# Seven products for eight: more mixed pairs in the second FFN, with their weight sums made during the first FFN

## The chip, the cores and the metric

The kernel runs on one core of one Trainium2 chip. The metric is the device time of one execution in microseconds (us). The engines are called PE (TensorE, matrix multiplies), PEld (its weight load), DVE (VectorE), ACT (ScalarE), POOL (GpSimd) and SP (SyncE, which issues most of the loads here).

## The reference, cut to what matters

One layer of a decoder on 256 tokens and 16 meta tokens, in fp32, with a model width of 2048. The change touches the last step of it, the second FFN:

```python
def swiglu(x, w_gate, w_up, w_down):
    return (jax.nn.silu(x @ w_gate) * (x @ w_up)) @ w_down
...
        h = h + 0.5 * swiglu(u, ffn1_w_gate[l], ffn1_w_up[l], ffn1_w_down[l])
        ... # projections, sparse attention, short convolution, merge
        u = rms_norm(h, ffn2_norm_g[l])
        h = h + 0.5 * swiglu(u, ffn2_w_gate[l], ffn2_w_up[l], ffn2_w_down[l])

    return h[:, N_META:]
```

`w_gate` and `w_up` are 2048 x 5632, `w_down` is 5632 x 2048. All weights arrive in fp32 from device memory, 4 bytes each.

## The kernel before, in words

**Three matmuls for one product.** PE works on rounded numbers (float32r). So each fp32 block of weights is split into a rounded part `whi` (made by ACT) and the rest `wlo` (DVE: the raw block minus `whi`), and each activation block likewise. A product is then a *trio* of matmuls: high times high, high times low, low times high. In the second FFN the activations (128 tokens) are PE's stationary operand and the weights, 512 columns wide, are the moving one.

**The stream of weights.** `Stream` holds all weights in the order of their use. A *raw tile* is 128 x 2048 fp32 (1 MB), loaded by SP into one of three buffers. `add` cuts it into *subs* of at most 1024 columns. `next` walks one sub further on PE. For sub number n it first has sub n + 3 split (`split`: ACT, then DVE), then runs the work whose turn has come (`later(fn, lag)`: the lag counts in subs), and then hands over the blocks of sub n. `whi` and `wlo` have four buffers each, so the split of a sub waits until PE has read the sub four places ahead of it. Since the program is written out in this order and each engine works through its own queue in order, this loop sets what stands behind what on ACT and DVE.

**The second FFN** (`ffn_tokens`) goes in two groups of 6 and 5 column blocks (`GROUPS`; 512 columns each). In a group, a *gate and up unit* f takes the 16 row blocks (k) of its 512 columns of gate and up, in 8 *pairs* of k. An ordinary pair is one raw tile, two subs, and 8 products (2 k, 2 token halves j, gate or up), so 24 matmuls. The products add up in four PSUM banks. A unit is followed, early in the next unit, by `gather` (sums from PSUM, then Silu on ACT), `times` (the product with up), `turn_blocks` (32 x 32 transposes on DVE), `move_blocks` (the blocks go out to device memory and back in another order, through POOL's queue), and `split_blocks` (the result into `mid`, high and low). The last unit of a group turns by `turn_columns` on DVE alone. After a group's units, `tokens` multiplies `mid` with the down weights, 512 output columns at a time (`d`), and `add` adds to the residual `ht`.

**Mixed pairs.** A pair named in `MIXED` is done as a 2 x 2 block product by Strassen and Winograd's scheme: 7 products instead of 8, so 21 matmuls instead of 24, for sums of the blocks on both sides. The sums of activations (`combos`, into `comb`) are made once. The sums of weights are made by DVE as the tile passes (`part`: two differences ahead of sub a, a sum and a difference ahead of sub b). The pair is then four subs, a to d, of 1024, 1024, 1024 and 512 columns. Four of the seven products add up in four more banks (`m`), which are the banks of the unit before, and `spread` adds these into `u` after the last mixed pair. Before, pairs 3 and 5 are mixed in every gate and up unit but the first, which has only 5; down has none.

Of the kernel before, what the change touches and what calls it, by code (L numbers as in the profile page):

```python
# [15 lines left out]
P = 128  # L16
# [49 lines left out]
MIXED = (3, 5)  # L66
# [3 lines left out]
class Stream:  # L70
# [66 lines left out]
    def part(self, raw, name):  # L137

        sub, add = self.nc.vector.tensor_sub, self.nc.vector.tensor_add
        b11, b12, b22, b21 = (raw[:, i * HALF : (i + 1) * HALF] for i in range(4))  # L140
# [49 lines left out]
def tile_decoder_layer(  # L190
# [50 lines left out]
    gu = down = 0  # L241
    for n in GROUPS:
        for i in range(gu, gu + 8 * n):
            if i % 8 in MIXED[i < 8 :]:
                st.add_mixed(wgu2[i])
            else:
                st.add(wgu2[i], 4, 512)
        chunks(wd2, down, down + 4 * n, 512)
        gu, down = gu + 8 * n, down + 4 * n
# [9 lines left out]
    ssq = [const.tile([P, T], F32, name=f"ssq{i}") for i in range(2)]  # L259
    R = const.tile([P, T], F32, name="R")  # L260
    R2 = const.tile([P, T], F32, name="R2")
# [96 lines left out]
    def quads(c, m, x, mixed, n, after_mixed):  # L358
# [5 lines left out]
        for i in range(n):  # L364
            k = 2 * i
            if i in mixed:
                s = [None, *(lambda part, q=q, i=i: mixed[i](q, part) for q in range(4))]
                plan.append([
                    [(c[1, 1], s[4], 0), (c[1, 0], of(k + 1, 1), 1)],
                    [(m[1], of(k, 1), 0), (m[5], s[1], 1)],  # L370
# [3 lines left out]
            else:  # L374
                plan.append([
                    [(c[j, q], of(k + u, j), q ^ u) for j in (1, 2) for q in ((0, 1), (1, 0))[u]] for u in range(2)
                ])
        flat = [id(p[0]) for steps in plan for unit in steps for p in unit]
        at = 0
        for i, units in enumerate(plan):  # L380
            for unit in units:
                blocks = [st.next()] + st.rest()
                for ps, xx, b in unit:
                    trio(ps, xx, blocks[b], id(ps) not in flat[:at], id(ps) not in flat[at + 1 :])
                    at += 1
            if i == max(mixed):
                after_mixed()
# [110 lines left out]
    def ffn_features():  # L498
# [3 lines left out]
        with tc.tile_pool(name="ffn1", bufs=2, reuse_waits="tile") as fp:  # L502
# [15 lines left out]

            two = [aux_tile(f"start{i}") for i in range(2)]
# [35 lines left out]
    def ffn_tokens():  # L555

        with ExitStack() as pools:
# [6 lines left out]
            comb = fp.tile([P, len(MIXED), 4, 2, P], F32R, name="comb")  # L564
            mixed = {i: lambda q, part, n=n: comb[:, n, q, part] for n, i in enumerate(MIXED)}
            late["junk"] = lambda: u[:, 0]

            def combos(n, i):
                y = st.mix[:, :HALF].rearrange("p (b j t) -> p b j t", b=2, j=2)
                z = st.mix[:, HALF : 2 * HALF].rearrange("p (q t) -> p q t", q=4)  # L570
                x = act[:, 2 * i : 2 * i + 2, :, LATER + META :].bitcast(F32).rearrange("p b i (j t) -> p b i j t", j=2)
# [5 lines left out]
                split_into(comb[:, n, :, 0], comb[:, n, :, 1], z)  # L577

            late["mt"] = lambda: fp.tile([P, 4, SEQ], F32, name="mt", bufs=2)
# [18 lines left out]
            def gather(c, s):  # L598
# [44 lines left out]
            for c, n in enumerate(GROUPS):  # L643
# [26 lines left out]
                if n % 2:  # L670
                    mm_tile(), mm_tile()
# [665 lines left out]
```

## Time and profile before

| | |
|---|---|
| median of 3 runs | 2132.63 us (2132.28 to 2132.64) |
| the profiled execution | 2132.57 us, its span 2130.8 us |
| granted PE clock | 1.0 |
| PE, DVE, ACT busy | 2123.0, 1418.4, 995.8 us |
| moved by DMA | 407.03 MB, 191 GB/s over the span |
| first FFN | up to about 796 us of the span |
| second FFN | from 1419 us on |

Read it so: busy time is the sum of the recorded durations on an engine. Matmuls overlap in the record (one lasts 389 ns with 512 columns, but the next starts after 227 ns), so PE's time is read from the distance of starts. A row of the timeline has the start, the duration, engine, line, operation, output and inputs, and in brackets how long the engine was idle before and who released it.

### The profile page before, as it was taken

The page shows a single profiled execution, that of the slowest core. Times are in us where ns is not written, and L with a number is a line of the kernel's source. Part 1 is how long each engine was busy: PE and PEld are TensorE (multiplying, and loading weights), DVE is VectorE, ACT ScalarE, POOL GpSimd, SP SyncE. Part 2 cuts the span into 40 slices and gives each one's busy share as a digit, 9 for nine tenths or more (in the row PEclk, how much of TensorE's full clock was granted, in tenths as well). Part 3 has the DMA queues.
Part 4 walks back from the last instruction along what each step waited for, and adds up shares of the span by engine and source line. Part 5 has one row for each costly group of instructions (what it writes and reads, how often), then busy time and mean ns, then how long its engine had stood idle before and what let it go on. Part 6 is the DMA issues. An engine that isn't in the chain of part 4 may idle for free.

```text
span 2130.8 us, 31133 instructions
## 1 busy us (share of the span) xinstructions
PE 2123.0 (100%) x12839; PEld 1909.7 (90%) x12839; DVE 1418.4 (67%) x1885; ACT 995.8 (47%) x1237; POOL 34.8 (2%) x73
## 2 busy tenths in 40 slices
PE   9999999999999999999999999999999999999999
PEld 9999999999999998799988888887888888888887
DVE  7555544455555556677677477898888854788863
ACT  6444433344444445455544444445555533455542
POOL 0000000000000000000000000000000000000000
PEclk9999999999999999999999999999999999999999
DMA  7554555555555555445455555555666655566664
GB/s 263 188 179 178 179 178 178 178 178 178 179 178 179 178 176 176 171 160 171 160 187 195 197 185 198 190 187 203 229 223 217 219 191 193 205 227 227 223 198 141
DMA packets 59935, 407.03 MB, mean 191 GB/s; under 512 B 7057, under 2 KB 7825, under 8 KB 12433
## 3 DMA queue, kind: packets, MB, share of 16 engines
q1 hardware_dynamic: 55872, 393.51, 53.5%
q0 software_dynamic: 3344, 10.49, 1.5%
q8 instruction: 100, 1.64, 0.3%
q10 hardware_dynamic: 576, 1.05, 0.1%
q14 instruction: 43, 0.34, 0.0%
HBM read 398.20 MB, written 6.82 MB: 190 GB/s over the span
## 4 chain that ended last, share of the span: by engine, by line
PE 97%; DVE 1%; DMA 1%; ACT 0%; issue 0%; SPq 0%; ACTq 0%
PE pd L322 4%; PE pd L320 4%; PE pd L321 4%; PE pg L321 4%; PE pu L321 4%; PE pu L322 4%; PE pg L322 4%; PE pg L320 4%; PE pu L320 4%; PE pd L349 4%; PE pd L348 4%; PE pd L350 4%; PE three L355 3%; PE three L356 3%; PE three L354 3%; PE pgt L350 3%
## 5 line engine op out<-in xcount | busy, mean ns | idle before, releaser
L129 DVE TENSOR_TENSOR wlo<-raw,whi 128x1024 fp32r<-128x1024 f32 (+1 forms) x749 | 909.5, 1219 | 664.8 <-ACT whi L128 661.0
L128 ACT ACTIVATE whi<-raw 128x1024 fp32r<-128x1024 f32 (+1 forms) x749 | 786.9, 1055 | 965.5 <-PE pd L321 146.2
L320 PE MATMUL pd<-mid,whi 128*128 128x272 f32 x704 | 201.7, 286 | 0.0
L321 PE MATMUL pd<-mid,whi 128*128 128x272 f32 x704 | 201.7, 286 | 0.0
L322 PE MATMUL pd<-mid,wlo 128*128 128x272 f32 x704 | 201.7, 286 | 0.0
L320 PE MATMUL pu<-act,whi 128*128 128x272 f32 x672 | 192.6, 287 | 0.0
L321 PE MATMUL pu<-act,whi 128*128 128x272 f32 x672 | 192.5, 287 | 0.0
L322 PE MATMUL pu<-act,wlo 128*128 128x272 f32 x672 | 192.5, 287 | 0.0
L320 PE MATMUL pg<-act,whi 128*128 128x272 f32 x672 | 192.5, 286 | 0.0
L321 PE MATMUL pg<-act,whi 128*128 128x272 f32 x672 | 192.5, 286 | 0.0
L322 PE MATMUL pg<-act,wlo 128*128 128x272 f32 x672 | 192.5, 286 | 0.0
L348 PE MATMUL pd<-whi,mid 128*128 128x512 f32 x352 | 136.9, 389 | 0.0
L349 PE MATMUL pd<-wlo,mid 128*128 128x512 f32 x352 | 136.9, 389 | 0.0
L350 PE MATMUL pd<-whi,mid 128*128 128x512 f32 x352 | 136.9, 389 | 0.0
L320 PEld LDWEIGHTS pd<-mid,whi 128*128 128x128 f32 x704 | 132.6, 188 | 0.0
L321 PEld LDWEIGHTS pd<-mid,whi 128*128 128x128 f32 x704 | 132.6, 188 | 0.0
L322 PEld LDWEIGHTS pd<-mid,wlo 128*128 128x128 f32 x704 | 132.6, 188 | 0.0
L320 PEld LDWEIGHTS pu<-act,whi 128*128 128x128 f32 x672 | 126.6, 188 | 0.0
L321 PEld LDWEIGHTS pg<-act,whi 128*128 128x128 f32 x672 | 126.6, 188 | 0.0
L322 PEld LDWEIGHTS pg<-act,wlo 128*128 128x128 f32 x672 | 126.6, 188 | 0.0
L320 PEld LDWEIGHTS pg<-act,whi 128*128 128x128 f32 x672 | 126.6, 188 | 0.0
L321 PEld LDWEIGHTS pu<-act,whi 128*128 128x128 f32 x672 | 126.6, 188 | 0.0
(299 smaller groups left out, 4216.3 us busy)
## 6 DMA issues: line engine op xcount, KB each, us to landing
raw<-in_wgu_dram SPq DMA_DIRECT2D x174, 1024.0 KB, 4.8
raw<-in_wd_dram SPq DMA_DIRECT2D x88, 1024.0 KB, 4.8
raw<-in_wcv_dram SPq DMA_DIRECT2D x24, 1024.0 KB, 4.8
raw<-in_wgc_dram SPq DMA_DIRECT2D x24, 1024.0 KB, 4.8
raw<-in_wga_dram SPq DMA_DIRECT2D x24, 1024.0 KB, 4.9
raw<-in_wo_dram SPq DMA_DIRECT2D x16, 1024.0 KB, 4.8
raw<-in_wqi_dram SPq DMA_DIRECT2D x8, 1024.0 KB, 4.8
raw<-in_wq_dram SPq DMA_DIRECT2D x8, 1024.0 KB, 4.8
```

What stands on the lines that cost most here:

```text
L128: nc.scalar.activation(hi[:, :n], raw, AF.Copy)
L129: nc.vector.tensor_sub(lo[:, :n], raw, hi[:, :n].bitcast(F32))
L320: nc.tensor.matmul(ps, whi, xhi, start=first, stop=False)
L321: nc.tensor.matmul(ps, whi, xlo, start=False, stop=False)
L322: nc.tensor.matmul(ps, wlo, xhi, start=False, stop=last)
L348: nc.tensor.matmul(ps, xhi, whi, start=k + i == 0, stop=False)
L349: nc.tensor.matmul(ps, xhi, wlo, start=False, stop=False)
L350: nc.tensor.matmul(ps, xlo, whi, start=False, stop=k + i == n - 1)
L354: nc.tensor.matmul(ps, x(0), w[0], start=first, stop=False)
L355: nc.tensor.matmul(ps, x(0), w[1], start=False, stop=False)
L356: nc.tensor.matmul(ps, x(1), w[0], start=False, stop=last)
```

## The change

1. In gate and up, pairs 1, 3 and 5 are mixed (before: 3 and 5). The first unit still mixes only pair 5. That makes 31 mixed pairs there, before 21.
2. The sums of weights of these 31 pairs are made during the first FFN. A `job` loads the raw tile through POOL's queue, DVE makes four sums in place (one after each of four subs), and POOL's queue stores the tile to a tensor `made` in device memory. A job starts every 7 subs, from sub 24 on. In the second FFN such a pair then comes as two raw tiles: three blocks of the weights as they are (0.75 MB; subs of 1024 and 512 columns) and the made tile (1 MB; two subs of 1024). `part` is no longer called for it.
3. Down is done by `quads` too, two column blocks at a time, with the four mixed products in the other four banks. Pairs 4, 6 and 8 of 12 are mixed in the first group, pairs 4 and 7 of 10 in the second, with the sums of weights made on the way (`part`). That is 2 x 3 + 2 x 2 = 10 mixed pairs. The sums of activations for them are made by `down_combos` about 21 subs after the unit that made these rows. `gather_down` and `half_to` take the place of `add`.
4. To make room, `s`, `xt` and a second `mt` are gone. `gather` writes into `few`, which is the storage of `ssq`, `R` and `R2`; it adds both token halves in one instruction of 1024 columns, before in two of 512. One of the four sums of activations of a mixed pair is written over the block it replaces, so `combos` splits its result in two pieces of 128 and 384 columns, before in one of 512.
5. In the last unit of down, the last pair takes its products bank by bank.

```diff
-MIXED = (3, 5)
+MIXED = 1, 3, 5
+FIRST_MIXED = 5,
+JOBS_FROM, JOBS_EVERY = 24, 7
+DOWN_MIXED = {6: (4, 6, 8), 5: (4, 7)}
...
+            if i % 8 in (FIRST_MIXED if i < 8 else MIXED):
+                made.append((i, scratch.tile([P, RAW], F32, name=f"made{i}")))
+                st.add(wgu2[i][:, HALF:], 3, 512)
+                st.add(made[-1][1], 4, 512)
...
+                if i in DOWN_MIXED[n]:
+                    st.add_mixed(wd2[down])
+                else:
+                    st.add(wd2[down], 4, 512)
...
+            def job(i, to, at):
+                box = {}
+                def load():
+                    box["x"] = fp.tile([P, RAW], F32, name="made", bufs=3)
+                    nc.gpsimd.dma_start(box["x"], wgu2[i])
...
+                st.later(load, at)
+                for n in range(4):
+                    st.later(lambda n=n: sums(n), at + JOBS_EVERY + n)
+                st.later(lambda: nc.gpsimd.dma_start(to, box["x"]), at + JOBS_EVERY + 4)
+            for at, (i, to) in enumerate(made):
+                job(i, to, JOBS_FROM + at * JOBS_EVERY)
...
-            def gather(c, s):
-                for j in (1, 2):
-                    nc.vector.tensor_add(s[:, j - 1], c[j, 0], u[:, j - 1])
+            def gather(x, c, box):
+                s = box["s"] = few.rearrange("p a t -> p (a t)")[:, :1024].rearrange("p (j c) -> p j c", j=2)
+                nc.vector.tensor_add(s, x, u[:, :2])
...
+                        for q, i in enumerate(i for i in DOWN_MIXED[n] if i // 2 == f):
+                            st.later(lambda i=i, n=n: down_combos(DOWN_MIXED[n].index(i), i), 21 + q)
...
-                for d in range(D // 512):
-                    pd = {j: mm_tile(f"pd{j}") for j in (1, 2)}
-                    tokens(pd, lambda k, j, part: mid[:, k, part, (j - 1) * P : j * P], 4 * n)
+                for d in (0, 2):
+                    x, c, m = banks()
+                    now = {i: down_sum(q, i) for q, i in enumerate(DOWN_MIXED[n])}
...
+                    quads(c, m, middle_tokens, now, 2 * n, after, g and d)
+                    st.later(lambda d=d, x=x, c=c, g=g: gather_down(d, x, c, g == 1))
```

DVE's queue at the start of the third gate and up unit of the first group, before: the four splits are those of subs 0 to 3 of the new unit, then come the sums from PSUM (`s`, `u`) of the unit that has just ended, the split of sub 4, `times`, the split of sub 5, the transposes, and sub 6, which is the first of a mixed pair (pair 3).

```order
L129 TENSOR_TENSOR wlo<-raw,whi 128x1024 x4
L600 TENSOR_TENSOR s<-three,u 128x512
L600 TENSOR_TENSOR s<-one,u 128x512
L602 TENSOR_TENSOR u<-three,u 128x512
L602 TENSOR_TENSOR u<-two,u 128x512
L129 TENSOR_TENSOR wlo<-raw,whi 128x1024
L608 SCALAR_TENSOR_TENSOR s<-u,rcol,s 128x512 x2
L129 TENSOR_TENSOR wlo<-raw,whi 128x1024
L614 STREAM_TRANSPOSE xt<-s 128x4x4x32 x2
L143 TENSOR_TENSOR mix<-raw 128x512
```

The same place on DVE in the changed kernel: subs 2 to 5 are now those of mixed pair 1.

```order
L132 TENSOR_TENSOR wlo<-raw,whi 128x1024 x3
L132 TENSOR_TENSOR wlo<-raw,whi 128x512
L665 TENSOR_TENSOR few<-three,u 128x1024
L667 TENSOR_TENSOR u<-one,u 128x512
L667 TENSOR_TENSOR u<-two,u 128x512
L132 TENSOR_TENSOR wlo<-raw,whi 128x1024
L674 SCALAR_TENSOR_TENSOR few<-u,rcol,few 128x512 x2
L132 TENSOR_TENSOR wlo<-raw,whi 128x1024
L682 STREAM_TRANSPOSE mt<-few 128x4x4x32 x2
L132 TENSOR_TENSOR wlo<-raw,whi 128x1024 x3
```

The rows keep their order, the split of sub 3 is half as wide, the first two sums are one, and the subs behind them are shorter on PE (1024, 512, 1024 and 1024 columns for 6, 3, 6 and 6 matmuls; before 12 each).

DVE at the start of the fifth unit of the first group, in the changed kernel: `mix` and the two rows after it are `down_combos`, between the splits of subs 1 and 2 of the unit. Before, nothing stood there, as in the third unit.

```order
L132 TENSOR_TENSOR wlo<-raw,whi 128x1024 x2
L624 TENSOR_TENSOR mix<-mid 128x512
L625 TENSOR_TENSOR mix<-mix 128x128
L626 TENSOR_TENSOR mix<-mix 128x128
L627 TENSOR_TENSOR mix<-mix 128x128
L628 TENSOR_TENSOR mix<-mix 128x128
L432 TENSOR_TENSOR mid<-mix,mid 128x128
L432 TENSOR_TENSOR below<-mix,below 128x3x128
L132 TENSOR_TENSOR wlo<-raw,whi 128x1024
L132 TENSOR_TENSOR wlo<-raw,whi 128x512
L665 TENSOR_TENSOR few<-three,u 128x1024
```

The sums of activations now stand ahead of the splits of subs 2 and 3 and of the sums from PSUM.

DVE at the start of down in the first group, before: from the split of sub 5 of the first down block on.

```order
L129 TENSOR_TENSOR wlo<-raw,whi 128x1024
L457 STREAM_TRANSPOSE mt<-s 32x2x4x32 x8
L129 TENSOR_TENSOR wlo<-raw,whi 128x1024
L457 STREAM_TRANSPOSE mt<-s 32x2x4x32 x8
L129 TENSOR_TENSOR wlo<-raw,whi 128x1024
L409 TENSOR_TENSOR mid<-mt,mid 128x4x256
L129 TENSOR_TENSOR wlo<-raw,whi 128x1024 x8
```

The same place in the changed kernel, where sub 8 is the first of mixed pair 4.

```order
L132 TENSOR_TENSOR wlo<-raw,whi 128x1024
L480 STREAM_TRANSPOSE mt<-few 32x2x4x32 x8
L132 TENSOR_TENSOR wlo<-raw,whi 128x1024
L480 STREAM_TRANSPOSE mt<-few 32x2x4x32 x8
L132 TENSOR_TENSOR wlo<-raw,whi 128x1024
L432 TENSOR_TENSOR mid<-mt,mid 128x4x256
L146 TENSOR_TENSOR mix<-raw 128x512
L147 TENSOR_TENSOR raw<-raw 128x512
L132 TENSOR_TENSOR wlo<-raw,whi 128x1024
L150 TENSOR_TENSOR mix<-mix,raw 128x512
L151 TENSOR_TENSOR mix<-raw,mix 128x512
L132 TENSOR_TENSOR wlo<-raw,whi 128x1024
```

Behind the transposes and the split of `mid`, the sums of weights of pair 4 now stand ahead of the splits of subs 8 and 9.

More of the change, by code (lines that the diff above doesn't have):

```diff
@@ L139, in part @@
         sub, add = self.nc.vector.tensor_sub, self.nc.vector.tensor_add
-        b11, b12, b22, b21 = (raw[:, i * HALF : (i + 1) * HALF] for i in range(4))
+        b12, b11, b22, b21 = (raw[:, i * HALF : (i + 1) * HALF] for i in range(4))
         t3, t2, t4 = (self.mix[:, i * HALF : (i + 1) * HALF] for i in range(3))
@@ L385, in quads @@
                     at += 1
+                blocks = [] if unit else blocks
             if i == max(mixed):
@@ L630, in split_blocks @@
                     split_into(hi, lo, x)
+            turns = [0]
             def banks():
[L633 to L641 removed]
@@ L643, in ffn_tokens @@
[L643 to L659 removed]
+                sides = []
@@ new lines, in banks, with out_columns @@
+                for _ in range(2):
+                    one, two = mm_tile("one"), mm_tile("two")
+                    sides.append((aux_tile("three"), one, two))
+                x, one, two = sides[turns[0] % 2]
+                c = {(1, 0): x[:, 0], (2, 0): x[:, 1], (1, 1): one, (2, 1): two}
+                y, six, seven = sides[1 - turns[0] % 2]
+                turns[0] += 1
+                return x, c, {1: y[:, 0], 5: y[:, 1], 6: six, 7: seven}
+            def out_columns(d, j):
+                queue = nc.gpsimd if st.n_loaded < len(st.loads) else (nc.sync, nc.scalar)[j - 1]
+                queue.dma_start(out[j - 1, :, d * 512 : (d + 1) * 512], ht[d][:, j - 1])
@@ new lines, in half_to, with gather_down @@
+            def half_to(to, x):
+                nc.vector.scalar_tensor_tensor(to, x, 0.5, to, op0=ALU.mult, op1=ALU.add)
+            def gather_down(d, x, c, last):
+                if not last:
+                    half_to(ht[d], x)
+                for j in (1, 2):
+                    for q in (0, 1) if last else (1,):
+                        half_to(ht[d + q][:, j - 1], c[j, q])
+                        if last:
+                            out_columns(d + q, j)
+            for g, n in enumerate(GROUPS):
+                for f in range(n):
+                    box = {}
+                    x, c, m = banks()
+                    if f == g == 0:
+                        rest = [i for i in MIXED if i not in FIRST_MIXED]
+                        for i, lag in zip((*FIRST_MIXED, *rest), (6, 15, 17)):
+                            st.later(lambda i=i: act_combos(i), lag)
+                    now = {i: mixed[i] for i in (MIXED if f or g else FIRST_MIXED)}
+                    quads(c, m, act_tokens, now, 8, lambda m=m: st.later(lambda: spread(m)), made=True)
+                    st.later(lambda x=x, c=c, box=box: gather(x, c, box))
+                    st.later(lambda box=box: times(box), 2)
```

140 lines of the change are left out of this document (80 added, 60 removed).

## The prediction, made before the changed kernel had run

> **What bounds the kernel now.** I read the page's parts first, then PE's waits, then busy time by stage.
>
> ```profile
> span 2130.8 us, 31133 instructions
> PE 97%; DVE 1%; DMA 1%; ACT 0%; issue 0%; SPq 0%; ACTq 0%
> ...
> PE three L355 <- DVE wlo L129: 1.5, 3, 0.8
> PE two L355 <- DVE wlo L129: 0.8, 1, 0.8
> ...
> 70.00:720.00 650.00, 650.00 (x5272) 650.00 (x5272) 339.63 (x409) 262.63 (x311) 0.32 (x1) 1.00 0.51 179
> 1440.00:1694.00 254.00, 251.78 (x1107) 206.96 (x1106) 220.83 (x278) 136.89 (x150) 13.92 (x25) 1.00 0.63 215
> ```
>
> The chain that ended last is 97% PE. In the second FFN PE waits only for DVE's low parts (`wlo`), 2.3 us in all. The last two rows are stretches (columns: length, busy PE, PEld, DVE, ACT, POOL, granted clock, DMA share, GB/s): most of the first FFN, where DVE is busy 339.63 of 650 us, and the first group's gate and up, where it is busy 220.83 of 254. So a matmul less is time won, as long as DVE, near its limit, delivers each split in time. The distance of matmuls:
>
> ```profile
> 1508.09 0.39 PE L354 MATMUL three<-whi,act 128*128 128x512 f32 x1
> 1524.41 0.39 PE L354 MATMUL three<-whi,comb 128*128 128x512 f32 x1
> ```
>
> The first opens the third gate and up unit (I call its time T0), the second the unit's first mixed pair, 3 ordinary pairs = 72 matmuls later: 16.32 / 72 = 0.2267 us each, 2.72 us for an ordinary sub of 12.
>
> **The matmuls that go.** 10 more mixed pairs in gate and up and 10 in down, each one product (3 matmuls) less: 60 x 0.2267 = 13.6 us, all on the path.
>
> **The first FFN.** The jobs add 124 DVE instructions of 128x512 at about 0.65 us (row 1518.39 below): 81 us, beside 310 us in which DVE is idle in the first stretch alone. They add 2.1 MB of DMA (a load and a store) per 7 subs. The stretch's row gives 650 / 5272 x 24 = 2.96 us a sub, so 101 GB/s beside 179, at a share of about 0.51 x 280 / 179 = 0.80. Weight loads are refilled two raw tiles ahead (about 11 us) and land in about 5 us (row `raw` below), and splits run three subs ahead, so I take 0; the ends are 0 and, if a job made PE wait 1 us, 31.
>
> **The first unit's waits.** Its one mixed pair loses its `part` on DVE.
>
> ```profile
> 1443.93 0.39 PE L354 MATMUL three<-whi,act 128*128 128x512 f32 x1
> 1444.76 0.50 PE L355 MATMUL three<-wlo,act 128*128 128x512 f32 x1 [0.44 <-DVE wlo L129]
> ...
> 1448.11 0.39 PE L354 MATMUL three<-whi,act 128*128 128x512 f32 x1
> ...
> 1450.02 0.50 PE L355 MATMUL three<-wlo,act 128*128 128x512 f32 x1 [0.85 <-DVE wlo L129]
> ...
> 1455.15 0.50 PE L355 MATMUL three<-wlo,act 128*128 128x512 f32 x1 [0.18 <-DVE wlo L129]
> ```
>
> From the first row to the last there are 34 matmuls, 7.7 us at the steady distance; they took 11.2, so 3.5 us are lost. After the wait at 1444.76, 14 matmuls take 3.35 us instead of 3.17: each wait also costs about 0.17 behind it. In the changed kernel the first wait stays (0.6, 0.1 more for the two-piece sums of activations, 0.17), and I estimate 0.7 behind it, where the root's small steps now stand between shorter subs. That saves 1.9; the ends are 0 and 3.5.
>
> **The start of a unit.** This decides. The rows are DVE's, then ACT's.
>
> ```profile
> 1509.38 1.23 DVE L129 TENSOR_TENSOR wlo<-raw,whi 128x1024 fp32r<-128x1024 f32 x1 [1.49 <-ACT whi L128]
> 1510.53 0.68 DVE L600 TENSOR_TENSOR s<-three,u 128x512 f32<-128x512 f32 x1
> ...
> 1513.57 1.23 DVE L129 TENSOR_TENSOR wlo<-raw,whi 128x1024 fp32r<-128x1024 f32 x1 [0.56 <-ACT whi L128]
> 1514.71 1.41 DVE L608 SCALAR_TENSOR_TENSOR s<-u,rcol,s 128x512 f32<-128x512 f32 x2
> 1516.03 1.22 DVE L129 TENSOR_TENSOR wlo<-raw,whi 128x1024 fp32r<-128x1024 f32 x1
> 1517.17 1.29 DVE L614 STREAM_TRANSPOSE xt<-s 128x512 f32<-128x512 f32 x2
> 1518.39 0.65 DVE L143 TENSOR_TENSOR mix<-raw 128x512 f32<-128x512 f32 x1
> ...
> 1519.68 1.22 DVE L129 TENSOR_TENSOR wlo<-raw,whi 128x1024 fp32r<-128x1024 f32 x1
> ...
> 1508.29 1.06 ACT L128 ACTIVATE whi<-raw 128x1024 fp32r<-128x1024 f32 x1 [1.66 <-PE one L356]
> 1511.24 1.34 ACT L604 ACTIVATE s<-s,rcol 128x512 f32<-128x512 f32 x2 [1.89 <-DVE s L600]
> 1512.49 1.04 ACT L128 ACTIVATE whi<-raw 128x1024 fp32r<-128x1024 f32 x1
> ...
> 1524.66 0.63 ACT L128 ACTIVATE whi<-mix 128x512 fp32r<-128x512 f32 x1 [1.66 <-PE one L356]
> ```
>
> Sub 3's high part starts 0.20 after T0, when PE has left the buffer. Then all is one chain: low part of sub 3, sums from PSUM, Silu on ACT, high part of sub 4 behind it in ACT's queue, its low part, `times`, sub 5, transposes, sub 6. From 1509.38 to 1518.39 it takes 9.01 us. Before, sub 6 has 16.3 us, so nobody waits.
>
> Now the changed kernel, from T0. Sub 3 has 512 columns: its high part takes 0.63, so its low part starts at 0.86 and the sums at 1.46. Their first half is one instruction of 1024 columns (1.22, as a split's), so Silu starts at 2.71; +1.25 high part of sub 4, 3.96; +1.08 its low part, 5.04; +1.14 `times`, 6.18; +1.32 sub 5, 7.50; +1.14 transposes, 8.64; +1.22 sub 6, 9.86; done +1.22, and PE sees it 0.05 later: 11.13. But pair 1 is mixed, so PE gets to sub 6 after 24 + 21 matmuls, and to its first `wlo` one later: 10.43. It waits 0.70, with what follows 0.87. Nine units have this start (not a group's first). Five are ordinary: 4.4 us.
>
> In three more (fifth and sixth of group one, fifth of group two) `down_combos` stands ahead of the split of sub 2. Its price is that of the sums of activations before:
>
> ```profile
> 1440.09 0.68 DVE L572 TENSOR_TENSOR mix<-act 128x512 f32<-128x512 f32 x1
> ...
> 1442.53 0.69 DVE L409 TENSOR_TENSOR comb<-mix,comb 128x512 fp32r<-128x512 f32 x1 [0.70 <-ACT comb L408]
> 1443.48 1.23 DVE L129 TENSOR_TENSOR wlo<-raw,whi 128x1024 fp32r<-128x1024 f32 x1 [0.26 <-ACT whi L128]
> ...
> 1500.11 0.68 DVE L593 TENSOR_TENSOR u<-one,u 128x512 f32<-128x512 f32 x1
> ...
> 1502.76 2.42 DVE L129 TENSOR_TENSOR wlo<-raw,whi 128x1024 fp32r<-128x1024 f32 x2
> ```
>
> 1443.48 - 1440.09 = 3.39, with two pieces on ACT 3.5. DVE is through with sub 1 at T0 - 3.0 (sub 3's place 1.29, less two subs, plus 1.14), so sub 2's low part starts at 0.5 and sub 3's at 1.64, 0.78 later than above: 0.70 + 0.78 + 0.17 = 1.65 each, 5.0. In the second unit of group one, two such sums and `spread` (1500.11 to 1502.76: 2.65) stand in a row. DVE is free for them at -8.4: 3.0 + 2.65 + two splits 2.3 + 3.5 + 1.14 + 0.6 bring the sums from PSUM to about 4.8, 3.3 late: 0.70 + 3.3 + 0.17 = 4.2.
>
> **The start of down.** The same chain with transposes on DVE, in the first group:
>
> ```profile
> 1676.93 1.06 ACT L128 ACTIVATE whi<-raw 128x1024 fp32r<-128x1024 f32 x1 [1.66 <-PE one L356]
> ...
> 1684.67 1.22 DVE L129 TENSOR_TENSOR wlo<-raw,whi 128x1024 fp32r<-128x1024 f32 x1
> ...
> 1694.30 1.23 DVE L129 TENSOR_TENSOR wlo<-raw,whi 128x1024 fp32r<-128x1024 f32 x1
> 1695.44 1.22 DVE L409 TENSOR_TENSOR mid<-mt,mid 128x1024 fp32r<-128x1024 f32 x1
> ```
>
> These are sub 3's high part, the low parts of subs 5 and 7 of down, then `mid`; T0 is 0.20 before the first row, 1676.73, so sub 7's low part starts at 17.57. In the changed kernel it is 0.35 later by `down_combos` (1.64 for 1.29) and 0.54 by the one sum: 18.46. Then `mid` 1.14 and 1.13, sums of weights 1.3, sub 8's low part 1.14, sums 1.3, sub 9's at 24.5, seen at 25.8. PE wants it after 8 x 12 + 6 + 1 matmuls, 23.35: 2.4 + 0.17 = 2.6, twice: 5.2. After that, mixed and ordinary pairs alternate as before in pairs 3 to 5 of gate and up, without a wait in the rows of PE. The end keeps its last sum and store.
>
> **Sum.** -13.6 - 1.9 + 4.4 + 5.0 + 4.2 + 5.2 = +3.3 us against the profiled execution's 2132.57 (its span and 1.8 us around it; 0.06 under the median): 2136.
>
> **Rivals.** *The weight loads and the blocks that move collide* (slower). The splits into `mid` wait on ACT for a round trip:
>
> ```profile
> 1518.76 0.56 POOL L621 DMA_DIRECT2D hold<-xt  x1 [32.74 <-DVE xt L614]
> 1525.00 2.19 POOL L624 DMA_DIRECT2D mt<-hold  x4 [5.68 <-PE one L356]
> ...
> mt<-hold POOLq DMA_DIRECT2D x36, 128.0 KB, 5.2
> raw<-in_wgu_dram SPq DMA_DIRECT2D x174, 1024.0 KB, 4.8
> ```
>
> From the transposes' end (9.9 in the changed kernel) + 0.3 + 6.2 + 1.6 + 5.2 the blocks are there at 23.2. ACT comes for them at about 22, behind sub 15's high part; the two pieces and sub 16's split then need 3.4, and PE wants that after 124 matmuls and the 0.87 lost, at 29.0. So PE waits if they come after 25.6. From 9 to 26 five weight loads (4.75 MB) run beside the 1 MB that moves: 6.0e6 bytes in 17 us, 350 GB/s, while 215 at a share of 0.63 means 341 at full share. If the two legs take 1.6 us longer each, the blocks come at 26.4: (0.8 + 0.17) x 9 = 9 us more, 2145. The Trainium skill ("DMA: Bandwidth & Descriptors", Bandwidth) puts the memory's limit for one core at about 358 GB/s; by that rule too the stretch is full, and the rival's time would be the same. For it speaks that the demand meets the rate; against it that 2.4 us are spare and that the stretch is short.
>
> *The splits come in time* (faster). If the chain at a unit's start is 0.7 us shorter than I walk it, the ordinary units cost nothing; if all starts hide, 2132.6 - 13.6 - 1.9 = 2117. For it: PE hardly waits today, with DVE as busy. Against: the chain is read row by row, and only 10.4 us are left for it. A half-way case lies at 2126.
>
> *The jobs disturb the first FFN* (slower): only if loads become twice as long or more; 1 us per job would give 2167.
>
> **Chances.** I take 0.2% (4.3 us) as what a measurement here can tell from no change. My sum: 0.58, of it 0.03 faster, 0.37 within, 0.18 slower, as its terms may each be off by a quarter (together about 3 us) and 2136.9 is near. Splits in time 0.17 faster; half way 0.06 (0.02 faster, 0.04 within). Collision 0.15, jobs 0.04, both slower. So 0.22, 0.41, 0.37. The sum's own range is 2130 to 2141. The whole range, from most of the splits in time to the collision, is 2119 to 2147.
>
> **What the profile would show.** PE with 60 rows less at the same distance; nine short waits for `wlo` at the first ordinary sub after mixed pair 1, largest in the second unit; two groups of waits near sub 8 and 9 of down's start; no waits in the first FFN; ACT's wait for `mid` short. Wrong I would be if PE's waits in the second FFN stay under 8 us, or if ACT waits for raw tiles or `mt` by several us.

## The result, and the profile after

The changed kernel takes 2158.21 us (median of 4 runs, 2151.47 to 2163.56), the kernel before 2132.64 us (4 runs beside them, 2132.28 to 2133.7). The ratio is 1.0119, with a 95% interval of 1.0107 to 1.0131: slower, and outside the predicted range of 2119 to 2147. The runs of the changed kernel lie 12 us apart, those of the kernel before 1.4 us. The profiled execution is the slowest of the four, 2163.56 us, 31.0 us over the 2132.57 of before.

From the page of the changed kernel, its span and the chain that ended last by engine:

```profile
span 2161.8 us, 31524 instructions
...
PE 86%; DVE 7%; DMA 4%; ACT 2%; issue 1%; POOL 0%; SPq 0%; DVEq 0%; ACTq 0%; POOLq 0%
```

Before, PE alone was 97% of that chain. Now 14% of it lie with others: DVE has 7%, and DMA, which had 1%, has 4%. Who PE waited for, and who ACT waited for (columns: the total in us, how often, the longest):

```profile
PE one L367 <- DVE wlo L132: 14.3, 21, 1.8
PE start L332 <- ACT whi L131: 4.8, 2, 4.4
PE three L367 <- DVE wlo L132: 4.0, 7, 0.8
PE one L366 <- ACT whi L131: 2.5, 3, 1.5
PE two L367 <- DVE wlo L132: 2.4, 3, 0.8
PE three L366 <- DVE few L665: 1.2, 1, 1.2
```

```profile
ACT whi L131 <- DMA raw<-in_wgu_dram: 61.8, 37, 4.1
ACT whi L131 <- DMA raw<-made: 23.5, 10, 4.3
...
ACT mid L431 <- DMA mt<-hold: 1.4, 4, 0.5
```

ACT's waits for raw tiles in the kernel before:

```profile
ACT whi L128 <- DMA raw<-in_wgu_dram: 2.3, 3, 1.4
```

PE waits for splits, as predicted. But two things have no term in the prediction's sum: `start`, the very first matmuls, and ACT's 85 us of waiting for raw tiles, before 2.3. ACT's wait for the moved blocks (`mt`), on which the prediction's rival was built, is 1.4 us.

The first FFN and the first group's gate and up as before, the second stretch 6 us longer (length, busy PE, PEld, DVE, ACT, POOL, granted clock, DMA share, GB/s):

```profile
70.00:720.00 650.00, 650.00 (x5273) 650.00 (x5272) 412.78 (x530) 262.86 (x312) 31.15 (x59) 1.00 0.75 274
1440.00:1700.00 260.00, 246.94 (x1050) 196.10 (x1049) 200.75 (x253) 141.89 (x169) 13.76 (x25) 0.99 0.74 255
```

In the first FFN the jobs cost PE nothing: 650 of 650 us, as before, with 73 us more of DVE and 95 GB/s more of traffic. In gate and up PE now stands still for 13 of 260 us, with DVE less busy than before.

**Where the 31.0 us are.** Distances of PE's starts against the steady 0.2267 us give: 60 matmuls less, -13.6; start-up, +5.8 (the first matmul of the second FFN has moved from 1419.45 to 1425.29); lost in the second FFN 39.8 by steps of over 0.09 us, before 3.4, so +36.4; the end, +0.8. That is 29.4. The other 1.6 us lie in smaller steps, which I did not assign. The 39.8 are about 1 in the first unit, 15.6 at the nine unit starts, 8.2 at the two starts of down, and about 15 inside the units, where the prediction's sum has nothing.

**One unit in the trace.** PE, then DVE, then ACT, in the fourth unit of the first group. The unit opens at T0 = 1560.62.

```profile
1560.62 0.39 PE L366 MATMUL one<-whi,act 128*128 128x512 f32 x1
...
1571.73 0.50 PE L367 MATMUL one<-wlo,act 128*128 128x512 f32 x1 [0.52 <-DVE wlo L132]
...
1581.61 0.39 PE L368 MATMUL three<-whi,act 128*128 128x512 f32 x1
1583.52 0.50 PE L366 MATMUL one<-whi,act 128*128 128x512 f32 x1 [1.52 <-ACT whi L131]
1584.78 0.80 PE L367 MATMUL one<-wlo,act 128*128 128x512 f32 x1 [0.76 <-DVE wlo L132]
1585.37 0.63 PE L368 MATMUL one<-whi,act 128*128 128x512 f32 x1
1585.80 0.63 PE L366 MATMUL three<-whi,act 128*128 128x512 f32 x1
...
1587.93 0.49 PE L368 MATMUL two<-whi,act 128*128 128x512 f32 x1
1588.26 0.39 PE L366 MATMUL three<-whi,act 128*128 128x512 f32 x1
```

```profile
1570.49 3.46 DVE L132 TENSOR_TENSOR wlo<-raw,whi 128x1024 fp32r<-128x1024 f32 x3
```

```profile
1577.28 1.06 ACT L131 ACTIVATE whi<-raw 128x1024 fp32r<-128x1024 f32 x1 [1.66 <-PE three L368]
1582.41 2.00 ACT L131 ACTIVATE whi<-raw 128x1024 fp32r<-128x1024 f32 x2 [4.07 <-DMA raw<-in_wgu_dram]
```

The wait at 1571.73 is the predicted one: DVE starts the split of sub 6 at T0 + 9.87 (predicted 9.86), and the start of that matmul comes 0.68 us late, with 0.11 behind it (predicted 0.70 and 0.17). The waits at 1583.52 and 1584.78 are not. ACT stood 4.07 us for a weight tile, PE lost 2.7 us, and then eight matmuls came 0.33 to 0.59 us apart, most of them 0.43, instead of 0.227: 1.7 us more. The transfers of that stretch, from POOL's and SP's queues, and the tile's own in the chain of waits:

```profile
1570.86 0.56 POOL L689 DMA_DIRECT2D hold<-mt  x1 [36.04 <-DVE mt L682]
1576.32 2.18 POOL L692 DMA_DIRECT2D mt<-hold  x4 [4.89 <-DMA hold<-mt]
```

```profile
1569.38 0.33 SPq L111 DMA_DIRECT2D raw<-made  x1
1572.84 2.06 SPq L111 DMA_DIRECT2D raw<-in_wgu_dram  x2
```

```profile
1572.84 9.47 DMA raw<-in_wgu_dram
```

A tile issued at 1572.84 landed 9.47 us later, beside another tile, a made tile and both legs of the blocks. ACT was free for it at 1578.34, 5.5 us after its issue. The median of such a load before was 4.8 us. The Trainium skill ("DMA: Bandwidth & Descriptors", Queues, rings and completion order) says that a DMA engine takes turns between the queues that have work for it; the row fits that, as a load on SP's queue takes twice its time while POOL's moves, but other loads on SP's own queue were on their way beside it, too.

**Start-up.** POOL's queue of the changed kernel, and the landing time of the load of weights that SP issues at 2.13 us in both kernels, first before, then after:

```profile
1.31 1.22 POOL L547 DMA_DIRECT2D made<-in_wgu_dram  x2 [0.37 <-issue]
```

```profile
DMA to landing us min/median/max: 5.1/5.1/5.1
```

```profile
DMA to landing us min/median/max: 10.5/10.5/10.5
```

The first job stands behind sub 24 in the program. On POOL nothing stood ahead of it that had to be waited for, so two loads of 1 MB left at 1.31 us, when the very first weights were on the way.

### The profile page after: what moved, and what is told of

The parts are those of the page before. It is cut to its first block, busy times and chain, and to the rows that moved or that the text cites. A ratio compares the mean times of both kernels' runs of the same rounds, so it can differ in the third digit from the quotient of the medians.

```text
span 2161.8 us, 31524 instructions
## 1 busy us (share of the span) xinstructions
PE 2126.3 (98%) x12779; PEld 1899.4 (88%) x12779; DVE 1531.1 (71%) x2060; ACT 1029.9 (48%) x1295; POOL 67.5 (3%) x135
## 3 DMA queue, kind: packets, MB, share of 16 engines
q10 hardware_dynamic: 576, 1.05, 0.1%
## 4 chain that ended last, share of the span: by engine, by line
PE 86%; DVE 7%; DMA 4%; ACT 2%; issue 1%; POOL 0%; SPq 0%; DVEq 0%; ACTq 0%; POOLq 0%
PE pd L334 4%; PE pd L332 4%; PE pd L333 4%; PE pu L333 4%; PE pg L333 4%; PE pu L334 4%; PE pg L334 4%; PE pg L332 4%; PE pu L332 4%; PE three L367 4%; PE three L368 4%; PE three L366 3%; DVE wlo L132 3%; PE pgt L361 3%; PE pgt L360 3%; PE pgt L362 3%
## 5 line engine op out<-in xcount | busy, mean ns | idle before, releaser
L132 DVE TENSOR_TENSOR wlo<-raw,whi 128x1024 fp32r<-128x1024 f32 (+1 forms) x811 | 961.9, 1198 | 584.7 <-ACT whi L131 580.2
L131 ACT ACTIVATE whi<-raw 128x1024 fp32r<-128x1024 f32 (+1 forms) x811 | 831.7, 1037 | 946.4 <-PE pd L333 146.2
L367 PE MATMUL three<-wlo,act 128*128 128x512 f32 x352 | 138.2, 393 | 3.4 <-DVE wlo L132 3.2
L366 PE MATMUL three<-whi,act 128*128 128x512 f32 x352 | 137.8, 392 | 1.2 <-DVE few L665 1.2
L368 PE MATMUL three<-whi,act 128*128 128x512 f32 x352 | 137.4, 390 | 0.0
L333 PEld LDWEIGHTS pu<-act,whi 128*128 128x128 f32 x672 | 126.6, 188 | 0.0
L334 PEld LDWEIGHTS pu<-act,wlo 128*128 128x128 f32 x672 | 126.6, 188 | 0.0
```

The lines of the kernel that those rows point to most:

```text
L131: nc.scalar.activation(hi[:, :n], raw, AF.Copy)
L132: nc.vector.tensor_sub(lo[:, :n], raw, hi[:, :n].bitcast(F32))
L333: nc.tensor.matmul(ps, whi, xlo, start=False, stop=False)
L334: nc.tensor.matmul(ps, wlo, xhi, start=False, stop=last)
L366: nc.tensor.matmul(ps, x(0), w[0], start=first, stop=False)
L367: nc.tensor.matmul(ps, x(0), w[1], start=False, stop=False)
```

## The experiments

The kernel before took 2132.1 to 2132.4 us beside each of them.

### Start-up and the round trip

First, the two causes that the traces name, one at a time and then together.

```diff
 # e1_paced_jobs: DVE holds the first two job loads
                     box["x"] = fp.tile([P, RAW], F32, name="made", bufs=3)
+                    if at < JOBS_FROM + 2 * JOBS_EVERY:
+                        nc.vector.memset(box["x"][:, :1], 0.0)
                     nc.gpsimd.dma_start(box["x"], wgu2[i])
```

> The changed kernel, but the loads of the first two jobs wait for a one-column memset of their buffer by DVE, which stands in DVE's queue where the job was meant to start (sub 24 and 31). Theory: these two loads of 1 MB ran at 1.3 us, because nothing in POOL's queue held them, and made the first weight loads late; everything up to the second FFN was 5.8 us later than before. Then the first FFN should start as in the kernel before, with no wait of several us on PE in the first 20 us, and the time be about 6 us below the changed kernel's (about 2152 against 2158). Rival: the late first loads were a chance of that execution; then the time stays within 2 us of the changed kernel's.

Measured: 2149.1 us (2144.43 to 2156.74), ratio 1.0083 (1.0059 to 1.0107). PE's 4.8 us for `start` are gone from its waits; of `start` this is left:

```profile
PE start L334 <- DVE wlo L132: 0.7, 1, 0.7
```

The second FFN starts at 1419.38 instead of 1425.29. So the loss at start-up was the early job loads. The medians differ by 9 us, more than the 5.8, but each of these kernels scatters over 12 us.

```diff
 # e3_no_round_trip: the blocks stay in the transposes' order
-                hold = hbm.tile([P, 4, 2, P], F32, name="hold")
-                nc.gpsimd.dma_start(hold, x)
-                rows = hold.rearrange("(r f) q j c -> q f r (j c)", r=4)
-                for q in range(4):
-                    nc.gpsimd.dma_start(x[q * 32 : q * 32 + 32], rows[q])
+                pass
```

> The changed kernel without move_blocks: the transposed blocks do not go out to device memory and back, and the splits into mid read them where they lie, so the blocks of nine of the eleven units are left in another order. Everything else is as in the changed kernel. Theory A (the 1 MB of the round trip crowds the weight loads of the mixed pairs): ACT's waits for raw tiles in gate and up nearly go, and with them PE's waits in the middle of units, 10 to 15 us in all, so about 2145. Theory B (the weight loads alone, 1.75 MB for each mixed pair, are too much): the waits stay within a third, less than 5 us gained.

Measured: 2141.8 us (2141.41 to 2142.7), ratio 1.0046 (1.0031 to 1.0061). The gain is 16 us, where 10 to 15 were expected, and the runs now lie 1.3 us apart. ACT's waits for raw tiles fall from 85 to 10 us:

```profile
ACT whi L131 <- DMA raw<-in_wgu_dram: 6.2, 5, 2.2
...
ACT whi L131 <- DMA raw<-made: 3.4, 1, 3.4
```

PE's waits inside the units are gone from the timeline, those at the unit starts stay: 0.68 + 0.11 at each ordinary one, 1.3 behind sums for down, 5.0 in the second unit, and about 2.2 at each start of down.

Both edits together are e5.

> The changed kernel with both edits that helped: the first two job loads wait for DVE, and the round trip of the blocks through device memory is left out (the blocks are split where the transposes left them, in another order). Theory: start-up and the crowded weight loads are all that the sum of the prediction lacked. Then the time is the sum's: 2141.8 us without the round trip, less the 5.8 us by which start-up came late in the profile = 2136, within 2 us. Rival: the two edits take away the same time, or there is a third loss of several us that the crowding only hides; then 2139 or more.

Measured: 2135.12 us (2134.48 to 2136.27), ratio 1.0013 (1.0004 to 1.0023). That is within the 2 us that were expected. So no third loss of several us hides behind the two: the sum of the prediction, 2136, is what the change costs without them.

### Is it the place, the bytes, or the lead?

Removing the round trip does not say what about it hurts. First, moving things in time.

```diff
 # e2_pairs_246
-MIXED = 1, 3, 5
-FIRST_MIXED = 5,
+MIXED = 2, 4, 6
+FIRST_MIXED = 6,
```

> The changed kernel with pairs 2, 4 and 6 mixed instead of 1, 3 and 5 (the first unit mixes pair 6 alone). The number of products and of sums is the same. Theory (DVE late at a unit's start): the sums from PSUM, Silu, times and transposes of the unit before now run beside two ordinary pairs more than they need, so the waits of the nine unit starts go: 15.4 us less in the profile, about 2143 us if nothing else changes. Rival (weight loads crowd each other, the starts only show it): mixed pairs alternate with ordinary ones just as before, so most of the waits only move; less than 5 us gained.

Measured: 2168.22 us (2163.84 to 2170.03), ratio 1.0164 (1.0147 to 1.0181). Missed by 25 us. With the last mixed pair at 6, one ordinary pair is left until the next unit needs the banks that `spread` empties, and PE waits there for `spread` (15 us in all); ACT still waits 58 us for raw tiles.

```diff
 # e7_paced_blocks_later: e1, and
-                        st.later(lambda box=box: move_blocks(box["x"]), 4)
-                        st.later(lambda to=to, box=box: split_blocks(to, box["x"]), 13)
+                        st.later(lambda box=box: move_blocks(box["x"]), 11)
+                        st.later(lambda to=to, box=box: split_blocks(to, box["x"]), 20)
 # e8_all_later: e7, and
-MIXED = 1, 3, 5
-DOWN_MIXED = {6: (4, 6, 8), 5: (4, 7)}
+MIXED = 2, 3, 5
+DOWN_MIXED = {6: (5, 7, 9), 5: (5, 7)}
 # e9_blocks_held: e8, and
+                nc.vector.tensor_copy(x[:, 0, 0, :1], x[:, 0, 0, :1])
                 nc.gpsimd.dma_start(hold, x)
```

> The whole change, with the first two job loads behind DVE, and the round trip of the blocks 7 subs later in the unit (at lag 11 instead of 4, their split at 20 instead of 13), where the loads that run are those of ordinary pairs. Theory: the crowding is one of place: mixed pairs load 1.75 MB each in 4.8 us of matmuls (385 GB/s), ordinary ones 1 MB in 5.4 us (193 GB/s), and the round trip stood among the mixed ones. Then nearly all of its cost goes: 2136 to 2139. Rival: the traffic of a whole unit is the limit (11.8 million bytes in 41.5 us, 284 GB/s); then the waits only move, and the time stays near the 2149 of the paced kernel, 2145 or more.

> The whole change with paced first jobs and the late round trip, the mixed pairs of gate and up at 2, 3, 5 instead of 1, 3, 5, and those of down at 5, 7, 9 and 5, 7. Theory: a second ordinary pair at a unit's start gives DVE's chain 5.4 us more for 4.8, and without sums of weights ahead; the nine waits at a unit's start (15 us in the profile) mostly go, and those at the start of down (8.6 us) too: from the 2137 of the late round trip to 2118 to 2124, faster than the kernel before. Rival: pairs 2 and 3 in a row ask for 3.5 MB in 9.5 us (385 GB/s), more than memory gave anywhere so far, and ACT waits for raw tiles by 1 to 2 us in each of ten units: 2130 to 2140.

> The kernel with paced first jobs, mixed pairs 2, 3, 5 and the round trip at lag 11, with one instruction more: a copy of one column of the block tile onto itself on DVE ahead of the first leg, so that POOL can only issue it when DVE is at lag 11. Without it the first leg left 11 us after a unit's start although it stands 7 subs later in the program, as POOL had nothing else to wait for. Theory: with the legs really at 20 to 34 us of the unit, beside the loads of ordinary pairs, the weight loads land in 5 to 6 us, ACT's waits for raw tiles (the 1 to 4 us in each unit and the slow matmuls behind them, about 30 of the 44 us lost) go: 2128 to 2134. Rival: two mixed pairs in a row starve the loads by themselves, with or without the round trip beside them; then 2145 or more.

Measured: 2157.86 (2156.63 to 2159.95; ratio 1.012, 1.0105 to 1.0135), 2158.52 (2155.33 to 2162.62; 1.0123, 1.0108 to 1.0139) and 2170.25 us (2164.93 to 2171.17; 1.0174, 1.0158 to 1.0189). All three missed. POOL's queue in e7 (third unit) and in e9 (fourth unit):

```profile
1522.82 0.56 POOL L691 DMA_DIRECT2D hold<-mt  x1 [36.20 <-DVE mt L684]
```

```profile
1577.15 0.56 POOL L692 DMA_DIRECT2D hold<-mt  x1 [33.60 <-DVE mt L691]
1586.29 2.18 POOL L695 DMA_DIRECT2D mt<-hold  x4 [8.58 <-DMA hold<-mt]
```

e7 repeats the mistake of start-up: seven subs later in the program, the leg still left right behind the transposes, 7.5 us after the unit's Silu, with nothing on POOL to hold it. So e7 and e8 did not test the place of the legs. In e8 the unit starts lost 0.6 us at most, but for the second unit, as expected of pairs 2, 3, 5; and 1.2 to 4.9 us came back in the middle of each unit, where ACT waited for raw tiles. In e9 the copy on DVE released the leg (`<-DVE mt L691`), 18.6 us after the Silu. It then took 8.6 us instead of 5, and ACT waited 94 us for raw tiles and 37 us for the blocks. A better place for the same bytes was not found, and mixed pairs 2 and 3 in a row stay bad.

Then bytes and lead, apart. A raw tile is loaded when the tile three places ahead of it has been split, so two tiles lie between. Two tiles of ordinary pairs are 48 matmuls, 10.9 us. The two tiles of a mixed pair, 0.75 MB and 1 MB, are 9 + 12 = 21 matmuls, 4.76 us, which is what one load takes alone.

```diff
 # e11_direct: e1, and one leg from tile to tile
-                ... (both legs, as in the diff of e3)
+                to = few.rearrange("p a t -> p (a t)")[:, :1024].rearrange("p (r j c) -> p r j c", r=4, j=2)
+                for r in range(4):
+                    for q in range(4):
+                        nc.gpsimd.dma_start(to[q * 32 : q * 32 + 32, r], x[r * 32 : r * 32 + 32, q])
 # e13_more_lead: e1, and a buffer of their own for the 0.75 MB tiles, with loads up to three tiles ahead
...
-            raw = self.raw_pool.tile([P, RAW], F32, name="raw")
+            if self.more and self.small(self.n_loaded):
+                raw = self.more.tile([P, 3 * HALF], F32, name="raw")
+            else:
+                raw = self.raw_pool.tile([P, RAW], F32, name="raw")
...
-            self.load(g + RAW_BUFS)
+            self.load(self.upto(g))
...
-DOWN_MIXED = {6: (4, 6, 8), 5: (4, 7)}
+DOWN_MIXED = {6: (4, 7), 5: (4, 7)}
```

> The changed kernel with paced first jobs, and the blocks moved in one leg from one tile of the core's own memory to another (16 transfers of 32 KB on POOL's queue) instead of two legs through device memory: 0.5 MB a unit instead of 1. Theory: ACT's waits for raw tiles come from the bytes that move beside the weight loads, so with half of them gone the time lies between 2149.1 (both legs) and 2135.1 (none), nearer the lower: 2136 to 2141. Rival: it is the small pieces or the second queue that disturb the loads, not the bytes; then 2145 to 2150.

> The changed kernel with paced first jobs and both legs through device memory, and one more buffer for the 0.75 MB weight tiles of mixed pairs, so that in gate and up loads run three tiles ahead instead of two. To make room, down of the first group has two mixed pairs (4, 7) instead of three, which gives up 6 matmuls, 1.4 us. Theory of the lead: two tiles ahead is 11 us of matmuls among ordinary pairs, but 4.8 us where one pair is mixed (9 + 12 matmuls), about what a load takes alone; so a load of 9 us is late, and with one tile more it isn't: 2149.1 + 1.4 - about 12 = 2136 to 2141. Rival, the rate: a unit asks for 11.8 million bytes in 41.5 us and memory doesn't give it; no lead helps then, and the time stays at 2147 to 2152.

Measured: e11 2141.77 us (2138.26 to 2143.12), ratio 1.0038 (1.0023 to 1.0052); e13 2139.87 us (2138.41 to 2142.87), ratio 1.0038 (1.0026 to 1.005). e11 came 0.8 us over its range, e13 within. In e13 the legs and their bytes are those of e1. What ACT waited for there, with the stretch of gate and up of e1 and of e13 (columns as above):

```profile
ACT whi L151 <- DMA raw<-in_wgu_dram: 5.2, 6, 2.3
```

```profile
1440.00:1700.00 260.00, 248.95 (x1068) 200.00 (x1067) 205.04 (x257) 146.62 (x170) 13.81 (x25) 0.99 0.74 257
```

```profile
1440.00:1700.00 260.00, 253.15 (x1099) 204.95 (x1098) 209.56 (x262) 147.21 (x169) 13.75 (x25) 1.00 0.71 256
```

The same 256 to 257 GB/s, but ACT's waits for raw tiles fall from 63 us to 5 (8 with down's) and PE is busy 4.2 us longer. ACT still waits 26 us for the blocks, and PE feels that at two places only (1.3 us at 1666, 1.2 at 1925). The loads did not become faster. From issue to landing in the same stretch, first e1, then e13:

```profile
DMA to landing us min/median/max: 4.1/5.5/11.4
```

```profile
DMA to landing us min/median/max: 4.2/6.6/9.4
```

So over the stretch memory gives the rate; what lacked was lead. For a part of each unit the rate is used up all the same. While the late tile of the unit above was on its way, the DMA engines were busy without a break (the second 1.00 is their share):

```profile
1572.84:1582.31 9.47, 9.16 (x41) 7.25 (x39) 4.16 (x4) 2.12 (x2) 2.18 (x4) 1.00 1.00 346
```

A longer lead bridges such a part. The rival, that memory doesn't give the rate of a whole unit, falls for pairs 1, 3, 5. In e11, half of the bytes beside the loads gave back about half of the 14 us between e1 and e5, so the bytes count too.

```diff
 # e12_direct_later: e11, the transposes one per sub, sums for down at lag 26 or 29, and
-MIXED = 1, 3, 5
-DOWN_MIXED = {6: (4, 6, 8), 5: (4, 7)}
+MIXED = 2, 3, 5
+DOWN_MIXED = {6: (5, 7, 9), 5: (5, 7)}
 # e14_direct_lead: e12 with the buffer of e13, and
-DOWN_MIXED = {6: (5, 7, 9), 5: (5, 7)}
+DOWN_MIXED = {6: (5, 8), 5: (5, 7)}
```

> The same, with mixed pairs 2, 3, 5 in gate and up, 5, 7, 9 and 5, 7 in down, the sums of activations for down at lag 26 or 29 and the last unit's transposes one per sub. Theory: without the crowding, what the mixed pairs at 2, 3, 5 did to the unit starts shows in the time (in the kernel with both legs the nine starts had lost 1 us instead of 15): 2122 to 2128, faster than the kernel before. Rival: two mixed pairs in a row starve the loads even with 0.5 MB a unit beside them; then 2136 or more.

> One leg, the later places of e12, and the extra buffer, with mixed pairs 5, 8 and 5, 7 in down. If bytes and lead both count, nothing is left but the first unit and the starts of down: 2132.4 - 12.2 (54 matmuls) + 3 to 7 = 2123 to 2127. If the places 2, 3, 5 starve the loads whatever the lead: 2134 or more.

Measured: 2155.2 us (2154.68 to 2155.39), ratio 1.0107 (1.0092 to 1.0122), and 2169.79 us (2162.75 to 2171.24), ratio 1.0169 (1.0153 to 1.0186). Both missed. With pairs 2 and 3 in a row ACT waits 48 us for raw tiles in e12, with one leg only, and 56 us in e14. But e14 does not test a longer lead. There is one buffer for the 0.75 MB tiles, so the tile of pair 3 can be loaded only when that of pair 2 has been split. SP's issue of pair 3's tile in the fifth unit, e12, then e14:

```profile
1598.48 0.33 SPq L111 DMA_DIRECT2D raw<-in_wgu_dram  x1
```

```profile
1612.34 0.33 SPq L131 DMA_DIRECT2D raw<-in_wgu_dram  x1
```

In e12 this is 2.4 us before ACT splits the first sub of pair 2 (1600.87), in e14 4.3 us after it (1608.08), and the loads behind it in SP's queue leave later too. At pairs 2 and 3 the buffer shortens the lead. Whether a second one would help was not run.

### Down alone

```diff
 # e4_down_only: gate and up as before, without jobs; down as in the change
-MIXED = 1, 3, 5
+MIXED = 3, 5
-                made.append((i, scratch.tile([P, RAW], F32, name=f"made{i}")))
-                st.add(wgu2[i][:, HALF:], 3, 512)
-                st.add(made[-1][1], 4, 512)
+                st.add_mixed(wgu2[i])
 # e6_down_only_later: e4, and
-DOWN_MIXED = {6: (4, 6, 8), 5: (4, 7)}
+DOWN_MIXED = {6: (5, 7, 9), 5: (5, 7)}
 # e10_down_only_spread: e6, and
-                            st.later(lambda i=i, n=n: down_combos(DOWN_MIXED[n].index(i), i), 21 + q)
+                            st.later(lambda i=i, n=n: down_combos(DOWN_MIXED[n].index(i), i), 23 if f < n - 2 else 27)
-                            st.later(lambda box=box, r=r: turn_columns(box["m"], box["s"], r), 3 + r // 2)
+                            st.later(lambda box=box, r=r: turn_columns(box["m"], box["s"], r), 3 + r)
```

> Down's ten mixed pairs alone: gate and up mix pairs 3 and 5 with their sums of weights made on the way, as in the kernel before (the first unit only 5), and there are no jobs and no made tiles; down is as in the changed kernel. Theory (loss from the mixed pairs in gate and up and from the jobs): PE has 30 matmuls less than before, 6.8 us, and pays for DVE being late at down's start in both groups, 3 to 5 us together; so 2129 to 2132, with no waits for raw tiles. Rival (down's mixed pairs cost much themselves): over 2140.

> No jobs, two mixed pairs in gate and up as before the change, and down mixed at pairs 5, 7, 9 and 5, 7 instead of 4, 6, 8 and 4, 7. Theory: at the start of down DVE is behind by transposes and the split of mid, and an ordinary pair gives it about 3 us back (5.4 us of matmuls, 2 splits of 1.14), so one ordinary pair more ahead of the first mixed one takes the waits away, some 8 to 9 us of the 2139.3 with the pairs at 4: 2130 to 2132, a little below the kernel before. Rival: it is the mixed pairs' own sums of weights that are too much, wherever they stand; the waits then move with the pairs and the time stays at 2137 to 2140.

> No jobs, mixed pairs of down at 5, 7, 9 and 5, 7, the sums of activations for down behind sub 5's split of a unit (lag 23) or ahead of the first mixed pair of down (27) instead of at a unit's start, and the four transposes of the last unit one per sub (1.8 us each) instead of two. Theory: the waits left with the pairs at 5 (three unit starts of 0.86, two starts of down of 0.86 + 2.1, 8.5 us in all) come from DVE's 2.8 us of sums of activations and 3.6 us of transposes between two splits, where PE takes 2.7 us a sub; they go, and the time is 2136.7 - 8.5 = 2128, faster than the kernel before. Rival: DVE is short of time over the whole of down (its mixed pairs need 4.9 us of DVE for 4.8 us of matmuls), and the waits come back at pairs 5 to 9: 2133 to 2137.

Measured: 2139.25 (2138.91 to 2140.07; ratio 1.0033, 1.002 to 1.0047), 2136.71 (2135.08 to 2137.33; 1.0018, 1.0008 to 1.0027) and 2134.55 us (2134.18 to 2135.46; 1.0011, 1.0002 to 1.0021). Each is better than the one ahead and each missed. In e4 a start of down loses 4.9 us, where the group saves 4.1 or 2.7 us of matmuls. In e6 3.0 are left, behind the two blocks of transposes. In e10 these are gone and 1.5 + 1.05 stand at the first mixed pair instead; the other three waits of 0.86 us, at a unit's first mixed pair, stay wherever the sums of activations stand. So in e10 the 6.8 us of matmuls saved in down are paid back: 5.1 at the first mixed pairs of down, where DVE makes sums of weights, and 2.6 at those three waits.

### The version that the runs point to

```diff
 # e15_all_made: e13's paced jobs and extra buffer, and
-MIXED = 1, 3, 5
-DOWN_MIXED = {6: (4, 6, 8), 5: (4, 7)}
+MIXED = 3, 5
+DOWN_MIXED = {6: (5, 7, 9), 5: (5, 7)}
...
-                    st.add_mixed(wd2[down])
+                    made.append((wd2[down], scratch.tile([P, RAW], F32, name=f"below{down}")))
+                    st.add(wd2[down][:, HALF:], 3, 512)
+                    st.add(made[-1][1], 4, 512)
```

It has e10's places for transposes and sums of activations as well.

> What the runs point to: gate and up keep two mixed pairs (3, 5), both with sums made in the first FFN, and down gets its mixed pairs (5, 7, 9 and 5, 7), with sums made in the first FFN too, so that DVE makes no sums of weights in the second FFN; 31 jobs as in the change, the first two paced; one buffer more for the 0.75 MB tiles; the last unit's transposes one per sub, the sums of activations for down at lag 23 and 27. The two legs of the blocks stay. Against the kernel before 30 matmuls less (6.8 us) and the first unit's waits down from 3.5 to about 1.6 us. Theory: with no mixed pair at the start of a unit, 1.5 us per sub of DVE's time free and three tiles of lead, no other wait comes back: 2132.2 - 6.8 - 1.9 + 1 (tail and second unit) = 2124 to 2127, faster than before. Rival: the alternation of mixed and ordinary pairs in down starves the loads, or the starts keep their waits of 1 to 2 us each: 2130 to 2134.

Measured: 2128.67 us (11 runs, 2127.55 to 2131.69) beside 2132.27, ratio 0.9984 (0.9975 to 0.9993): faster than the kernel before by 3.6 us, and 1.7 us over its range. Nearly all of PE's waits for splits in its second FFN are these:

```profile
PE one L389 <- DVE wlo L152: 1.8, 3, 0.8
PE one L388 <- ACT whi L151: 1.2, 2, 0.7
```

By distances PE loses 4.9 us there, 3.7 of them at two places (1621 and 2003), where it waits for ACT's high part first. ACT itself waits there for the moved blocks (2.0 and 2.2 us), and just ahead of that for a made tile (3.5 and 2.3): with the other waits gone, the late blocks of the prediction's rival do show.

## Why the prediction was wrong, point by point

- **The lead of the loads: the step that failed.** "Weight loads are refilled two raw tiles ahead (about 11 us) and land in about 5 us" was used for the first FFN, where it holds. It was not asked again for the second FFN, and there both figures fail: where a pair comes as a short and a made tile the lead is 4.8 us, and beside the round trip a load took up to 11.0 us. The sum had no term for it. The trace of before had a warning that its median of 4.8 us hides: one load beside the round trip, issued at 1523.39, took 9.0 us to land. It did no harm, as ACT split that tile only at 1536.44, 4.0 us after it had landed. Runs with and without the round trip give the size: 2149.1 - 2135.1 = 14 us between medians, 9 to 22 over the runs of e1. e13 shows that with more lead most of it goes, while the loads land no sooner.
- **The collision as a rival** had the right partners, and the load was there as computed: five loads and the two legs, 346 GB/s at a share of 1.00, where 350 against 341 was computed. (That is not the most that memory gives this core: at start-up, from 12 to 17 us, the changed kernel moved 416 GB/s, more than the limit that the prediction cites.) But it let the blocks be late, whose 2.4 us to spare held (ACT waited 1.4 us for them in all), and it priced 1 us a unit. The victim was the weight tile, which had nothing to spare, so 2145 was too low.
- **"So I take 0" for the first FFN** held for the FFN itself: no wait, 274 GB/s at a share of 0.75 for the predicted 280 at 0.80. It failed ahead of it, by 5.8 us: I read sub 24 in the program as a time, and on a queue with nothing to wait for it is none. The rival of disturbing jobs spoke of 1 us per job and did not see this either.
- **Matmuls and the steady distance** held. **Ordinary starts** were predicted at 0.87 and measured at 0.79. **The second unit** was 4.2, measured 4.6. **Starts behind sums for down** were 1.65; measured 1.3, 3.1 and 2.6, and 1.3 each in e1, e3 and e5. **The first unit** lost about 1.0 where 1.6 was left for it.
- **The starts of down**: 2.6 each, measured 3.5 and 4.7, and 2.2 each in e1, e3 and e5. The extra stands in the slowest execution of the changed kernel; at the second start a halved clock behind a wait is part of it, and the rest was not traced to a cause.
- **"The end keeps its last sum and store"** was 0.8 us short: the sums of the last four banks are the end now, not of one.

With what the sum had left out taken away, the kernel runs at 2135.1 us against 2136. So the terms that were there came out, in sum, within 1 us. That it is so close is partly luck: in e5 the predicted terms together come out about 2 us lower than predicted, and the end and small steps, which the sum lacked, bring about 1 us back. And the sign of failure that the prediction named was the right one: ACT waits for raw tiles, 85 us in all.

## What to carry to other kernels

Count a prefetch in time, not in buffers: whenever a change makes a tile last shorter, multiply it out again, and compare with the landing time under the traffic that the change adds, with the longest and not with the median. For every transfer that a change issues, ask what on its own queue it must wait for; where nothing does, it starts at once, whatever stands ahead of it in the program. Work taken off the bound engine must be paid somewhere with room: DVE at the starts of units and of down had none, the first FFN had.

## What the runs showed of the hardware that I had not expected

After the waits at 1583.52 and 1584.78 (1.52 and 0.76 us idle within 3.2 us) the granted clock was halved for three microseconds (columns as in the other rows of stretches; the clock is the 0.50):

```profile
1585.00:1588.00 3.00, 3.00 (x8) 2.32 (x9) 2.51 (x3) 2.65 (x4) 0.00 (x0) 0.50 0.41 96
```

That is the 1.7 us behind the wait, over half of its own 2.7. Single waits of 0.7 us did not do it; one of 1.84 us at 2068.11 did. The Trainium skill ("TensorE: Matmul & The Clock Gate", Part 1) has two clocks, half and full, and lets the half one return after an idle window of about 3.4 us. The half clock is what the row shows; but no gap in the second FFN of the changed kernel was longer than 1.84 us, so here less is enough. The length of the gaps does not settle it: in e1 gaps of 1.44 and 0.76 us (at 1576.03 and 1577.29) left the clock at 1.00, and gaps of 0.96 and 0.76 us (at 1621.22 and 1622.48) halved it:

```profile
1577.50:1580.50 3.00, 3.00 (x14) 2.42 (x14) 2.34 (x3) 2.38 (x4) 0.00 (x0) 1.00 0.58 169
1624.00:1627.00 3.00, 3.00 (x8) 2.32 (x8) 1.59 (x2) 2.53 (x4) 0.00 (x0) 0.50 0.96 339
```

The second surprise is the scatter: 12 us between runs of the changed kernel and of e1, 1.3 us once the round trip was out. Late loads alone do not make it, since the runs of e12, where ACT waits 48 us for tiles, lie 0.7 us apart. Its cause stays open.
